# Softmax maxima of two of four heads by pairs of 64-row products, in groups of four, with scores and maxima in one ring of five PSUM banks

## The chip, the core and the metric

The kernel runs on one core of one Trainium2 chip. The metric is the time of one execution on the device in microseconds (us). The core has one engine for matrix products (TensorE, PE in the profile, with its weight loads as PEld) and three others that work on whole tiles: VectorE (DVE), ScalarE (ACT) and GpSimd (POOL). SyncE (SP) issues most DMAs. Each engine takes its instructions in the order in which they were written, and waits on semaphores for the others. PSUM, where TensorE writes, has eight banks of 128 partitions by 512 fp32 values.

## What is computed

One layer of a hybrid backbone: a modulated RMSNorm, one input projection, then grouped-query softmax attention (8 query heads, 2 key heads, head size 64) and, beside it, a bidirectional gated linear recurrence with 4 heads; an output projection, and a SwiGLU feed-forward layer. There are 2048 latent tokens and 256 context tokens, so attention runs over 2304 keys. What matters here is

```
def block(q):
    s = jnp.einsum('bqkgd,bnkd->bkgqn', q, keys).astype(jnp.float32) * scale
    p = jax.nn.softmax(s, axis=-1)
    return jnp.einsum('bkgqn,bnkd->bqkgd', p.astype(vals.dtype), vals)
```

The softmax subtracts a number per query and head from the scores before the exponential. In exact arithmetic the result does not depend on that number, as long as it is near the row's maximum.

## The kernel before

The kernel has an opening and the projection (to 709 us of the profile), the stage that holds attention and the recurrence together (to some 1620 us), and then the output projection and the feed-forward layer. The change lies in the second stage, and prepares for it in the first.

**Items and steps.** Attention runs over 32 items: for each of the two key heads (`g`) 16 blocks of 128 queries (`qt`), each with four query heads side by side, 512 columns. An item has 18 steps, one for each tile of 128 keys (`NKT` is 18). The loop at line 1407 counts `x` over all steps; `n` is the item and `k` the step in it.

**Operands in two parts.** Queries and keys are split into a high part that keeps fewer bits and a low part that holds the rest. `KS[g]` holds the keys, 64 rows of high part and under them 64 rows of low part; `qa` holds the high part of the queries twice, in both halves of the rows, so one 128-row product gives high query times whole key. `KB` holds the high part of the keys alone (rows 0 to 63) and a row of -1, `qb` the low part of the queries and, in that row, the maxima. The halves of the keys are made in `qk_side` (lines 590 to 603), written to `s_k`, and read by `load_kb` (line 1263) with one DMA for each third of the keys.

**A step.** `scores` (line 1182) takes a bank of `ps_st` (three banks, tag "s"), puts two 128x512 products into it (lines 1190 and 1191), and lets ACT take the exponential into `p` (line 1194). Then `chunk` (line 1151) makes a piece of the maxima that the next but one or the next item will need: a 128x512 product into a bank of `ps_mx` (two banks, tag "x") and on DVE the minimum along the row into `mn` (lines 1159 to 1161; signs are turned, so minima stand for maxima). An item has 18 chunks: 16 for the four heads by four blocks of 512 latent keys, and two (16 and 17) for the last 256 keys of two heads each. `CHUNKS` (line 1383) puts them at steps -10 to 7 of the item before, which is step 8 to 17 of the one before that and 0 to 7. With chunk 17 the twenty minima become four (`neg`, line 1171). At step 10 `maxima` (line 1173) turns `neg` with TensorE into a bank of the same pool (`pn`), ACT copies it to `mr`, and four DMAs put it into `qb`.

**A batch.** At step 10 an item's first batch, and at step 2 of the next item its second (`EVENTS`, line 1130), the loop at line 1488 first lets the recurrence compute a level (`rec.round`, products `pa`, line 818), then DVE adds one pair of exponentials (`SUMS`, letter E), then TensorE makes the products with the values and the sums (`products`, lines 1215 and 1223, tile `av`), and after that DVE does the masked copies of the level (line 831) and POOL its multiplications (`M`, `Q`, `C`, lines 847 to 855). Two POOL additions of 128x1024 go with each batch (line 1205).

**The recurrence.** Its work is placed by hand: `Recurrence` (line 995) gives every operation a step `x`, for head `h` at 18 x (4+7h) plus a fixed number (lines 739 to 743 and 1004 to 1029). So the stage repeats every seven items, and within the seven the steps carry different work. `level_context` (line 1050) does one level of the context's unit: a copy by ACT from `C` to `M` (line 844) and two multiplications by POOL.

**Order.** In the stage the orders of PE, DVE, ACT and POOL are those of the program (line 1460); only SP's is planned.

Of the kernel before, what the change touches and what calls it, by code (L numbers as in the profile page):

```python
# [38 lines left out]
P5M = False  # L39
WOV = (1, 3, 5, 7)  # L40
# [27 lines left out]
def block_kernel(ctx: ExitStack, tc: tile.TileContext, a: dict, out: bass.AP, dbg=None):  # L68
# [240 lines left out]
    with proj as st:  # L309
# [223 lines left out]
        def qk_side(t, c):  # L533
# [56 lines left out]
            else:  # L590
                sf = qp.tile([P, 512], F32R, tag="sk", name=f"s{name}", bufs=SK)
                sk = sf[:, :256].rearrange("p (g s d) -> p g s d", g=2, s=2)
                nc.scalar.activation(sk[:, :, 0, :], x, AF.Copy)
                nc.vector.tensor_tensor(sk[:, :, 1, :], x, f32v(sk[:, :, 0, :]), op=ALU.subtract)
# [118 lines left out]
    with ExitStack() as st:  # L713
# [413 lines left out]

        BATCHES = [[0, 8], [8, 18]]
# [3 lines left out]
        class Item:  # L1132
# [18 lines left out]
            def chunk(self, c):  # L1151

                if c == 0:
                    self.mn = sm.tile([P, 4, 5], F32, tag="mn", name=f"mn{self.nm}")
                s = ps_mx.tile([P, 512], F32, tag="x", name=f"mx{self.nm}_{c}")
                K = KS[self.g]
                if c < 16:
                    h, k = divmod(c, 4)
                    nc.tensor.matmul(s, self.qa[:, h * P:(h + 1) * P], K[:, k * 512:(k + 1) * 512],  # L1159
                                     start=True, stop=True)  # L1160
                    nc.vector.tensor_reduce(self.mn[:, h, k:k + 1], s, axis=AX.X, op=ALU.min)  # L1161
                else:
                    h = (c - 16) * 2
                    for i in range(2):
                        nc.tensor.matmul(s[:, i * 256:(i + 1) * 256], self.qa[:, (h + i) * P:(h + i + 1) * P],
                                         K[:, 2048:], start=True, stop=True)
                    nc.vector.tensor_reduce(self.mn[:, h:h + 2, 4], s.rearrange("p (h k) -> p h k", h=2),
                                            axis=AX.X, op=ALU.min)
                if c == 17:
                    self.neg = sm.tile([P, 4], F32, tag="neg", name=f"neg{self.nm}")  # L1170
                    nc.vector.tensor_reduce(self.neg, self.mn, axis=AX.X, op=ALU.min)

            def maxima(self):

                pm = ps_mx.tile([P, 512], F32, tag="x", name=f"pn{self.nm}")
                nc.tensor.transpose(pm[:4, :P], self.neg, ident)
# [5 lines left out]
            def scores(self, k):  # L1182
# [5 lines left out]
                s = ps_st.tile([P, 512], F32, tag="s", name=f"s{nm}")  # L1188
# [60 lines left out]
        QB = [qpl.tile([P, 512], F32R, name=f"qb{i}") for i in range(2)]  # L1249
        one32 = kvp.tile([P, 32], F32, name="one32")  # L1250
# [12 lines left out]
        def load_kb(g, r):  # L1263
            n = NTOK // 3
            nc.sync.dma_start(f32v(KB[r][:64, :]), s_k[g][:64, r * n:(r + 1) * n])
# [63 lines left out]
        def turn_heads(t, hs, eng, lag=0, ps=ps_h, tag="h"):  # L1329

            pt = ps.tile([P, 512], F32, tag=tag, name=f"mt{t}_{hs[0]}")
# [4 lines left out]
        def turn_first():  # L1336

            turn_heads(FIRST, [0, 1, 2], nc.vector, 1, ps_mx, "x")
            split_mix(FIRST, mixed[FIRST][0][:, :512], 0, 4, nc.gpsimd)
# [43 lines left out]
        CHUNKS = [-10, -9, -8, -7, -6, -5, -4, -3, -2, -1, 0, 1, 2, 3, 4, 5, 6, 7]  # L1383
        chunks, loads = {}, {}
        for n in range(1, NIT):
            for c in range(18):
                chunks.setdefault(NKT * (n - 1) + CHUNKS[c], []).append((n, c))

# [14 lines left out]
        for x in range(CHUNKS[0], 0):  # L1403
            for n, c in chunks.pop(x, ()):
                items[n].chunk(c)

        for x in range(NKT * NIT + 1):
# [65 lines left out]
            for m, c in chunks.pop(x, ()):  # L1473
                items[m].chunk(c)
# [13 lines left out]
            for e, t in enumerate(EVENTS):  # L1488
                m, r = divmod(x - t, NKT)
                if r or m < 0:  # L1490
                    continue
                made = rec.round() if e in ROUNDS else iter(())
                next(made, 0)
                for p in range(BATCHES[e][0] // 2, BATCHES[e][1] // 2):
                    if SUMS[p] in "EQ":
                        items[m].add(p)
                items[m].products(e)
# [3 lines left out]
                if TE == 9 and e in ROUNDS:  # L1501
                    for u in rec.lanes.values():
                        u.extend(u.lv)

# [701 lines left out]
```

## Time and profile before

| what | us |
|---|---|
| median of 3 runs | 3114.13 (3111.4 to 3115.98) |
| profiled execution | 3117.9 |
| its span, first to last instruction | 3116.1 |

The page of the profile adds up what each engine was busy. A window gives the same for a stretch of time. The groups give for one line and operation the count, the busy time and the mean duration of one; records of PE overlap, as the next product enters while the last one leaves, so what a product costs is read from the distance of two starts. The timeline gives instructions in order of time, neighbours of one kind merged, with the idle time in front and what ended it in square brackets. The view of waits adds up who waited for whom.

### The profile page before, as it was taken

Reading aid. Unit: us, or ns where it says so; the run is one execution under the profiler, and the core shown is the slowest. Engines: PE = TensorE matmul, PEld = TensorE weight load, DVE = VectorE, ACT = ScalarE, POOL = GpSimd, SP = SyncE. Lnnn points to the kernel's source line nnn. Section 1 sums busy time; section 2 is a strip of 40 time slices with the busy share of each in tenths; the row PEclk is TensorE's granted clock in tenths of the full one; section 3 lists DMA queues with packets and bytes.
Section 4 is the critical chain, followed back from the end, with each engine's and each line's share of the span. In section 5 each row is a group of like instructions: output and inputs, shape, how many; then the busy total and the mean of one; then the engine's idle time right before and its main releaser. Section 6 shows DMA issues by size and latency. Waiting matters only on the chain.

```text
span 3116.1 us, 51235 instructions
## 1 busy us (share of the span) xinstructions
PE 3074.8 (99%) x18844; PEld 2483.8 (80%) x18844; DVE 1845.9 (59%) x3252; ACT 1303.1 (42%) x2656; POOL 1602.7 (51%) x1291
## 2 busy tenths in 40 slices
PE   9999999999999999999999999999999999999999
PEld 7888888886777778777778878788888788888887
DVE  4554655427777787786745574544478743333567
ACT  4422322214545545555553253333345533333454
POOL 3311212106989888898862118676600277776122
PEclk9999999999999999999999999999999999999999
DMA  7544544425111212111124444656596533333765
GB/s 244 159 139 127 155 139 150 141 69 138 42 38 49 67 53 71 39 52 48 42 83 147 129 142 155 213 176 211 171 331 196 182 118 106 102 102 102 254 195 196
DMA packets 372998, 410.77 MB, mean 132 GB/s; under 512 B 34469, under 2 KB 264073, under 8 KB 372234
## 3 DMA queue, kind: packets, MB, share of 16 engines
q1 hardware_dynamic: 369722, 405.06, 41.0%
q8 instruction: 148, 2.42, 0.3%
q10 hardware_dynamic: 3024, 2.43, 0.2%
q14 instruction: 104, 0.85, 0.1%
HBM read 277.54 MB, written 133.97 MB: 132 GB/s over the span
## 4 chain that ended last, share of the span: by engine, by line
PE 70%; DVE 7%; DMA 5%; POOL 3%; issue 2%; ACT 1%; SPq 1%; POOLq 0%; DVEq 0%; ACTq 0%
PE pA L1785 13%; PE av L1215 7%; PE pB L1785 6%; PE y L1355 6%; PE pd0A L2082 4%; PE pd1A L2082 3%; PE s L1190 3%; PE s L1191 3%; PE pC L1785 3%; PE mx L1159 3%; PE i L442 2%; DVE mn L1161 2%; PE pd0B L2082 2%; PE pd1B L2082 2%; PE pa L818 2%
## 5 line engine op out<-in xcount | busy, mean ns | idle before, releaser
L1194 ACT ACTIVATE p<-s 128x512 f32<-128x512 f32 x576 | 338.2, 600 | 372.6 <-PE s L1191 358.1
L1161 DVE TENSOR_REDUCE mn<-mx 128x1 f32<-128x512 f32 x496 | 337.0, 689 | 175.2 <-PE mx L1159 172.3
L1215 PE MATMUL av<-p,VS 128*64 128x256 f32 x2304 | 259.9, 379 | 0.0
L1190 PE MATMUL s<-qa,K 128*128 128x512 f32 x576 | 244.1, 424 | 1.2 <-ACT p L1194 1.0
L1191 PE MATMUL s<-qb,KB 128*128 128x512 f32 x576 | 226.9, 394 | 0.0
L1215 PEld LDWEIGHTS av<-p,VS 128*64 128x64 f32 x2304 | 160.4, 137 | 75.3 <-issue 1.1
L1205 POOL TENSOR_TENSOR ps<-p,p 128x1024 f32<-128x1024 f32 x64 | 153.4, 2396 | 101.8 <-ACT p L1194 101.7
L1159 PE MATMUL mx<-K,qa 128*128 128x512 f32 x496 | 200.1, 404 | 2.4 <-DVE mn L1161 1.2
L435 PE MATMUL f<-hTh,wh 128*128 128x512 f32 (+1 forms) x640 | 188.1, 373 | 0.2 <-ACT ft L475 0.2
L1205 POOL TENSOR_TENSOR ps<-ps,p 128x1024 f32<-128x1024 f32 x64 | 153.1, 2392 | 12.0 <-ACT p L1194 10.6
L2019 DVE TENSOR_TENSOR dl<-dl,x 128x512 fp32r<-128x512 f32 x154 | 113.8, 765 | 66.5 <-ACT x L2012 64.9
L2012 ACT ACTIVATE x<-dl 128x512 fp32r<-128x512 f32 x154 | 95.9, 631 | 95.4 <-DMA dl<-s_hid0S 37.7
L852 POOL TENSOR_TENSOR Q<-Q,T 128x512 f32<-128x512 f32 x96 | 131.3, 1383 | 8.1 <-PE pa L818 7.7
L435 PEld LDWEIGHTS f<-hTh,wh 128*128 128x128 f32 x640 | 116.9, 190 | 20.4 <-ACT ft L475 0.3
L1190 PEld LDWEIGHTS s<-qa,K 128*128 128x128 f32 x576 | 109.0, 189 | 27.0 <-issue 12.3
L2012 ACT ACTIVATE dh<-dl 128x512 fp32r<-128x512 f32 x154 | 88.9, 624 | 98.7 <-PE pd1A L2082 42.2
L2019 DVE TENSOR_TENSOR dl<-dl,dh 128x512 fp32r<-128x512 f32 x154 | 105.5, 697 | 39.9 <-ACT dh L2012 37.7
L1159 PEld LDWEIGHTS mx<-K,qa 128*128 128x128 f32 x496 | 93.6, 189 | 38.0 <-DVE mn L1161 15.3
L131 POOL TENSOR_TENSOR rs_xf<-ms_xf,mhalf 128x1 f32<-128x1 f32 x16 | 9.9, 620 | 221.1 <-DVE ms_xf L129 218.5
L1191 PEld LDWEIGHTS s<-qb,KB 128*128 128x128 f32 x576 | 109.3, 190 | 14.9
L435 PE MATMUL f<-hTl,wh 128*128 128x512 f32 (+1 forms) x320 | 118.7, 371 | 0.0
L131 POOL TENSOR_TENSOR rs_qq<-ms_qq,mhalf 128x4 f32<-128x4 f32 x32 | 34.0, 1061 | 161.0 <-DVE ms_qq L129 160.3
(436 smaller groups left out, 8913.5 us busy)
## 6 DMA issues: line engine op xcount, KB each, us to landing
w<-in_w_gu_dram SPq DMA_DIRECT2D x88, 512.0 KB
wm<-in_w_mod_dram SPq DMA_DIRECT2D x24, 1024.0 KB
dl<-s_wT SPq DMA_DIRECT2D x88, 256.0 KB
dl<-s_wB SPq DMA_DIRECT2D x66, 256.0 KB
wq<-in_w_down_dram SPq DMA_DIRECT2D x44, 256.0 KB
s_wT<-wq SPq DMA_DIRECT2D x44, 256.0 KB
dl<-s_hid1S SPq DMA_DIRECT2D x44, 256.0 KB
dl<-s_hid0S SPq DMA_DIRECT2D x44, 256.0 KB
```

The lines of the kernel that those rows point to most:

```text
L435: nc.tensor.matmul(pm[:, :n], w[wi][:, k, c0:c0 + P], hT[b][hi][:, k, :], start=(k == 0 and i == 0), stop=(k == KT - 1 and i == 2))
L1159: nc.tensor.matmul(s, self.qa[:, h * P:(h + 1) * P], K[:, k * 512:(k + 1) * 512], start=True, stop=True)
L1161: nc.vector.tensor_reduce(self.mn[:, h, k:k + 1], s, axis=AX.X, op=ALU.min)
L1190: nc.tensor.matmul(s, KS[self.g][:, ks], self.qa, start=True, stop=False)
L1191: nc.tensor.matmul(s, KB[k // 6][:, k % 6 * P:(k % 6 + 1) * P], self.qb, start=False, stop=True)
L1194: nc.scalar.activation(self.pairs[p][:, o:o + 512], s, AF.Exp, scale=-1.0)
L1205: (nc.gpsimd if SUMS[p] in "PQ" else nc.vector).tensor_tensor(t, a, self.pairs[p], op=ALU.add)
L1215: nc.tensor.matmul(self.av[i * 64:(i + 1) * 64, :256], VS[k // 6][:, k % 6, :], self.pairs[k // 2][:, o:o + 256], start=(k == 0), stop=(k ...
L1355: nc.tensor.matmul(py, m[:, k, :], wo[k][w][hf], start=(k == 0 and i == 0), stop=(k == KT - 1 and i == 2), skip_group_check=True)
L1785: nc.tensor.matmul(acc, w[wi][:, k, :], x[xi][k], start=(start and k == 0 and i == 0), stop=(stop and k == KH - 1 and i == 2), skip_group_ ...
L2019: nc.vector.tensor_tensor(lo, f32v(lo), f32v(hi), op=ALU.subtract)
L2082: nc.tensor.matmul(cur[t], l[:, t * P:(t + 1) * P], r, start=(start and j == 0 and f == 0), stop=(stop and j == NHF - 1 and f == 2), skip_ ...
```

## The change

- In `qk_side` the two halves of the keys of a tile are written in turned order for some tiles: `flipped(t)` is 1 for tiles 4 to 7, 12 to 15 and 17. In `KS` the high part then stands in rows 64 to 127 for every second block of 512 latent keys, and for the last tile. `load_kb` reads each run of tiles with one order by a DMA of its own: 7 for 3.
- For chunks 0 and 1, now one for each of heads 0 and 1, four products of 64 rows take the place of four of 128: rows 0 to 63 for blocks 0 and 2, rows 64 to 127 for blocks 1 and 3, each into a bank of its own. They hold high query times high key alone. For heads 2 and 3 and for the last 256 keys the chunks (8 to 17) stay as they were.
- A group of four is issued at step 10 (chunk 0) and at step 2 (chunk 1), in front of the recurrence's products and the batch. Its four reductions on DVE come behind the batch's add and in front of the masked copies. The other ten chunks go to steps 12 to 17 and 4 to 7; steps 0, 1, 3, 8, 9 and 11 have none. The first item with maxima has its own list.
- Scores, maxima and `pn` take banks in turn from one ring of five (`bank`), in the order st, x, st, x, st.
- The reduction to four minima goes to the step after chunk 17, into the first four columns of a 128x128 tile, and `pn` is turned in full width.

```diff
+def flipped(t):
+
+    return t // 4 % 2 if t < 16 else t % 2
...
-                nc.scalar.activation(sk[:, :, 0, :], x, AF.Copy)
-                nc.vector.tensor_tensor(sk[:, :, 1, :], x, f32v(sk[:, :, 0, :]), op=ALU.subtract)
+                f = flipped(t)
+                nc.scalar.activation(sk[:, :, f, :], x, AF.Copy)
+                nc.vector.tensor_tensor(sk[:, :, 1 - f, :], x, f32v(sk[:, :, f, :]), op=ALU.subtract)
...
+        taken = [0]
+
+        def bank(name):
+
+            n = taken[0] = taken[0] + 1
+            pl, tag = ((ps_st, "s"), (ps_mx, "x"))[n % 5 % 2]
+            return pl.tile([P, 512], F32, tag=tag, name=name)
...
-                s = ps_mx.tile([P, 512], F32, tag="x", name=f"mx{self.nm}_{c}")
                 K = KS[self.g]
+                if c < 2:
+                    banks = [bank(f"mx{self.nm}_{c}{i}") for i in range(4)]
+                    for i, s in enumerate(banks):
+                        r = slice(i % 2 * 64, i % 2 * 64 + 64)
+                        nc.tensor.matmul(s, self.qa[r, c * P:(c + 1) * P], K[r, i * 512:(i + 1) * 512],
+                                         start=True, stop=True)
+                    return [(self.mn[:, c, i:i + 1], s) for i, s in enumerate(banks)]
+                s = bank(f"mx{self.nm}_{c}")
...
-                if c == 17:
-                    self.neg = sm.tile([P, 4], F32, tag="neg", name=f"neg{self.nm}")
-                    nc.vector.tensor_reduce(self.neg, self.mn, axis=AX.X, op=ALU.min)
+                if c == LAST_CHUNK:
+                    later(1, self.lowest)
+
+            def lowest(self):
+
+                nc.vector.tensor_reduce(neg_all[:, :4], self.mn, axis=AX.X, op=ALU.min)
...
-                pm = ps_mx.tile([P, 512], F32, tag="x", name=f"pn{self.nm}")
-                nc.tensor.transpose(pm[:4, :P], self.neg, ident)
+                pm = bank(f"pn{self.nm}")
+                nc.tensor.transpose(pm[:, :P], neg_all, ident)
...
-                s = ps_st.tile([P, 512], F32, tag="s", name=f"s{nm}")
+                s = bank(f"s{nm}")
...
         def load_kb(g, r):
-            n = NTOK // 3
-            nc.sync.dma_start(f32v(KB[r][:64, :]), s_k[g][:64, r * n:(r + 1) * n])
+            t0 = 6 * r
+            while t0 < 6 * r + 6:
+                t1 = t0
+                while t1 < 6 * r + 6 and flipped(t1) == flipped(t0):
+                    t1 += 1
+                rows = slice(64 * flipped(t0), 64 * flipped(t0) + 64)
+                nc.sync.dma_start(f32v(KB[r][:64, (t0 - 6 * r) * P:(t1 - 6 * r) * P]), s_k[g][rows, t0 * P:t1 * P])
+                t0 = t1
...
-        CHUNKS = [-10, -9, -8, -7, -6, -5, -4, -3, -2, -1, 0, 1, 2, 3, 4, 5, 6, 7]
+        CHUNKS = [(-8, 0), (2, 1)] + list(zip((-6, -5, -4, -3, -2, -1, 4, 5, 6, 7), range(8, 18)))
+        FIRST_CHUNKS = [(-1, c) for c in range(8, 17)] + [(2, 0), (6, 1), (7, 17)]
+        LAST_CHUNK = 17
...
+        def lowest(group):
+
+            for o, s in group or ():
+                nc.vector.tensor_reduce(o, s, axis=AX.X, op=ALU.min)
...
-            for m, c in chunks.pop(x, ()):
-                items[m].chunk(c)
+            if k not in (2, 10):
+                for m, c in chunks.pop(x, ()):
+                    lowest(items[m].chunk(c))
...
+                group = [v for i, c in chunks.pop(x, ()) for v in items[i].chunk(c)]
                 made = rec.round() if e in ROUNDS else iter(())
                 next(made, 0)
                 for p in range(BATCHES[e][0] // 2, BATCHES[e][1] // 2):
                     if SUMS[p] in "EQ":
                         items[m].add(p)
+                lowest(group)
                 items[m].products(e)
                 next(made, 0)
```

More of the change, by code (lines that the diff above doesn't have):

```diff
@@ L1249, in block_kernel @@
         QB = [qpl.tile([P, 512], F32R, name=f"qb{i}") for i in range(2)]
+        neg_all = kvp.tile([P, P], F32, name="neg")
+        nc.gpsimd.memset(neg_all, 0.0)
         one32 = kvp.tile([P, 32], F32, name="one32")
@@ L1327, in split_mix, with turn_heads @@
             eng.tensor_tensor(ml[:, k0:k1, :], pv, f32v(hv), op=ALU.subtract)
-        def turn_heads(t, hs, eng, lag=0, ps=ps_h, tag="h"):
-            pt = ps.tile([P, 512], F32, tag=tag, name=f"mt{t}_{hs[0]}")
+        def turn_heads(t, hs, eng, lag=0, pt=None):
+            if pt is None:
+                pt = ps_h.tile([P, 512], F32, tag="h", name=f"mt{t}_{hs[0]}")
             for i, h in enumerate(hs):
@@ L1336, in turn_first @@
         def turn_first():
-            turn_heads(FIRST, [0, 1, 2], nc.vector, 1, ps_mx, "x")
+            turn_heads(FIRST, [0, 1, 2], nc.vector, 1, bank(f"mt{FIRST}_0"))
             split_mix(FIRST, mixed[FIRST][0][:, :512], 0, 4, nc.gpsimd)
@@ L1382, in block_kernel @@
         extra.setdefault(X0 + 10, []).append((turn_first, ()))
[L1383 removed]
+        CHUNKS = [(-8, 0), (2, 1)] + list(zip((-6, -5, -4, -3, -2, -1, 4, 5, 6, 7), range(8, 18)))
+        FIRST_CHUNKS = [(-1, c) for c in range(8, 17)] + [(2, 0), (6, 1), (7, 17)]
+        LAST_CHUNK = 17
         chunks, loads = {}, {}
         for n in range(1, NIT):
[L1386 to L1387 removed]
+            for x, c in CHUNKS if n > 1 else FIRST_CHUNKS:
+                chunks.setdefault(NKT * (n - 1) + x, []).append((n, c))
         rec = Recurrence()
@@ L1402, in block_kernel @@
             load_v(0, r)
-        for x in range(CHUNKS[0], 0):
+        for x in range(-1, 0):
+            now[0] = x
             for n, c in chunks.pop(x, ()):
                 items[n].chunk(c)
+            for f, args in todo.pop(x, []):
+                f(*args)
+        def lowest(group):
+            for o, s in group or ():
+                nc.vector.tensor_reduce(o, s, axis=AX.X, op=ALU.min)
         for x in range(NKT * NIT + 1):
@@ L1503, in block_kernel @@
                         u.extend(u.lv)
+            for m, c in chunks.pop(x, ()):
+                lowest(items[m].chunk(c))
     with ExitStack() as st:
```

2 lines of the change are left out of this document (1 added, 1 removed).

## The prediction

> **What bounds the kernel now.** First the page's span, then the busy time of two stretches (columns: stretch and its length, then busy us of PE, PEld, DVE, ACT and POOL, instructions in brackets; then granted clock, DMA), then PE in order of time, then the waits.
>
> ```profile
> span 3116.1 us, 51235 instructions
> ```
>
> ```profile
> 780.00:1560.00 780.00, 775.16 (x7409) 592.93 (x7406) 599.84 (x977) 408.04 (x920) 689.25 (x559) 1.00 0.18 50
> 709.40:726.20 16.80, 15.08 (x48) 9.64 (x46) 14.19 (x23) 8.14 (x13) 4.25 (x2) 0.80 0.73 164
> ```
>
> In the attention stage (780 to 1560) PE is the bound, but POOL is close: 689 of 780 us, 88%. The second row is the stage's start, where PE idles and the granted clock falls to 0.80. The stage has 32 items of 18 steps, a step being one key tile; here is the end of the run of steps 3 to 10 in item 14, up to the recurrence's products `pa`, which open the batch:
>
> ```profile
> 1114.50 0.39 PE L1190 MATMUL s<-qa,K 128*128 128x512 f32 x1
> 1114.73 0.40 PE L1191 MATMUL s<-qb,KB 128*128 128x512 f32 x1
> 1114.96 0.40 PE L1159 MATMUL mx<-K,qa 128*128 128x512 f32 x1
> 1115.45 0.27 PE L1176 MATMUL pn<-identr,neg 128*4 128x128 f32 x1
> 1115.65 1.15 PE L818 MATMUL pa<-Q,M 128*64 128x64 f32 x32
> ```
>
> A record lasts 0.39, but the next starts 0.23 later: a 128x512 product costs 0.23 us of PE, and a step with a maximum 0.70. From the step's second score product (1114.73) to `pa` are 0.92 us, with 0.49 between `mx` and `pn` where 0.23 would do. DVE is the pace beside it. From the view of who waited for whom, PE's weight loads in the same stretch (us in total, times, longest):
>
> ```profile
> PEld mx L1159 <- DVE mn L1161: 9.6, 34, 0.6
> ```
>
> **The change, part by part.** I write A for the group that goes in at step 10 and B for that at step 2.
>
> *Pairs.* Eight 64-row products replace eight of 128 rows. No 64-row product is in this trace. The nearest row is the batch's group, with busy us and mean ns:
>
> ```profile
> L1215 PE MATMUL av<-p,VS 128*64 128x256 f32 x1968 | 221.8, 379 | 0.0
> ```
>
> 1968 records in 221.8 busy us are 0.113 each while one lasts 0.379, so two column halves run together. The other bound is that they take turns at 0.23. I take pairs of 0.23, as `av` is the nearest shape: per item 8 slots become 4, 0.92 us less; at the other bound nothing. [...] What a change of shape costs stands here:
>
> ```profile
> 1102.78 0.40 PE L1159 MATMUL mx<-K,qa 128*128 128x512 f32 x1
> 1103.10 1.15 PE L818 MATMUL pa<-Q,M 128*64 128x64 f32 x32
> ```
>
> 0.32 instead of 0.23 is 0.09 a switch; a group adds one in front, as the one to `pa` is paid already. For the signal that releases a bank I take 0.05 (POOL to ACT it is 0.02 below: 1176.64 to 1176.66).
>
> *The ring, and the new wait.* Five banks go round over scores, maxima and `pn`. At step 10 the order is score 10, `pn`, four maxima. So **the fourth product takes the bank of score 10, and waits for that step's exponential**; at step 2 the fourth waits for the exponential of step 1. Behind it on PE stand the rest of the group, `pa` and the whole batch, and POOL's `Q` and DVE's masked copy wait for `pa`. Before, `pa` needed none of these exponentials. When do they end? ACT in order of time, first in item 14, then in item 18:
>
> ```profile
> 1115.22 0.60 ACT L1194 ACTIVATE p<-s 128x512 f32<-128x512 f32 x1 [0.15 <-PE s L1191]
> ...
> 1225.90 1.10 ACT L1194 ACTIVATE p<-s 128x512 f32<-128x512 f32 x2
> ```
>
> An undisturbed one starts 0.49 after the second score product (1114.73) and takes 0.60; two in a row follow at 0.50.
>
> Plain A, from the second score product: the exponential ends at 1.09, the fourth product starts at 1.14, `pa` at 1.14+0.32 = 1.46 against 0.92. The run before it has lost the maxima of steps 3, 8 and 9, 0.69. Net -0.15 us. Plain B: step 1's exponential ends at -0.46+0.49+0.03+0.60 = 0.66, the fourth product starts at 0.71, `pa` at 1.03 against 0.23+0.32 = 0.55; steps 11, 0 and 1 lose 0.69. Net -0.21. Had PE not to wait, the fourth product would start at 0.23+0.20+0.23 = 0.66 in A (0.20 from `pn` to the next shape, as 1115.45 to 1115.65) and at 0.32+0.23 = 0.55 in B: -0.63 and -0.37.
>
> *Where ACT is held.* In some items POOL is late, and ACT, which takes its instructions in order, waits for POOL in front of exponential 10. So far nothing on PE stood behind that. ACT's row in the view of waits (780 to 1560), then item 16: POOL, ACT and PE in order of time:
>
> ```profile
> ACT M L844 <- POOL C L855: 16.4, 7, 6.3
> ```
>
> ```profile
> 1166.31 2.39 POOL L1205 TENSOR_TENSOR ps<-p,p 128x1024 f32<-128x1024 f32 x1 [3.60 <-ACT p L1194]
> ...
> 1176.22 0.42 POOL L855 TENSOR_TENSOR C<-M,T 128x128 f32<-128x128 f32 x1
> ```
>
> ```profile
> 1176.66 0.31 ACT L844 ACTIVATE M<-C 128x128 f32<-128x128 f32 x1 [3.11 <-POOL C L855]
> 1176.88 0.58 ACT L1194 ACTIVATE p<-s 128x512 f32<-128x512 f32 x1
> ```
>
> ```profile
> 1174.01 1.19 PE L818 MATMUL pa<-Q,M 128*64 128x64 f32 x28
> ```
>
> POOL begins at 1166.31, released by exponential 3, and reaches the context's `C` 9.9 us later; PE was at `pa` after 7.7. Exponential 10 ends at 1177.46, 3.45 after `pa` began. With the change `pa` waits for it: 1177.46+0.05+0.32 = 1177.83, **3.8 us later**. Nothing that the change removes lies in that POOL chain. The plan (line 1005) places a head's work at 18 x (4+7h) plus fixed steps, so it repeats every 7 items: 9, 16 and 23, 3 x 3.8 = 11.4. Three waits of 3.1 and the longest, 6.3 in item 2, make 15.6 of the row's 16.4. Item 2 and three smaller kinds, each with `pa` on PE and exponential 10 on ACT:
>
> ```profile
> 777.59 1.49 PE L818 MATMUL pa<-Q,M 128*64 128x64 f32 x32
> ...
> 782.92 0.59 ACT L1194 ACTIVATE p<-s 128x512 f32<-128x512 f32 x1
> ...
> 1143.80 1.19 PE L818 MATMUL pa<-Q,M 128*64 128x64 f32 x32
> ...
> 1144.12 0.59 ACT L1194 ACTIVATE p<-s 128x512 f32<-128x512 f32 x1
> ...
> 1210.15 1.04 PE L818 MATMUL pa<-Q,M 128*64 128x64 f32 x28
> 1210.35 0.59 ACT L1194 ACTIVATE p<-s 128x512 f32<-128x512 f32 x1
> ...
> 1226.75 1.15 PE L818 MATMUL pa<-Q,M 128*64 128x64 f32 x32
> ```
>
> Item 2: 783.51+0.37-777.59 = +6.3. Items 1, 8, 15, 22 (the context's preparation stands before exponential 10): it ends at 1144.71, comes some 0.6 earlier with shorter steps, so 1144.11+0.37-1143.80 = +0.7, four times 2.8. Items 10, 17, 24 (an output at step 9): 1210.94-0.69+0.37-1210.15 = +0.5, three times 1.5. Items 4, 11, 18, 25 have `psf` between score 10 and `pn`, no wait: 0.92 less, 0.46+0.09 more, -0.4 each, -1.6. The 15 plain A give -2.3. **A: +18.1.** B: 27 plain -5.7; three (into items 11, 18, 25, with an output's squares on ACT) like item 18, where the two exponentials from 1225.90 end at 1227.00 and `pa` came at 1226.75: 1227.00-0.23+0.37-1226.75 = +0.4, +1.2. **B: -4.5.**
>
> *DVE.* Its count stays; four reductions stand together behind the batch's own add, some 2.6 us, in front of the masked copies. They lie beside the batch. DVE's last before, and the next run's first score, at A in item 14:
>
> ```profile
> 1119.65 0.26 DVE L873 TENSOR_REDUCE T<-T 128x64 f32<-128x128 f32 x1
> 1120.77 0.50 PE L1190 MATMUL s<-qa,K 128*128 128x512 f32 x1
> ```
>
> DVE was done at 1119.91; with 2.6 more at 1122.5, and the next run's first maximum, of step 12, is there 1.0+0.4 after its first score, at 1122.2: nothing with two banks to spare, 0.3 a group where the cover is gone. Of the 9.6 us that weight loads waited for reductions I take 3 away (0 to 9.6), since steps 8 to 11 and 0 to 3 have none.
>
> *Start, loads, the rest.* The start is paced by DVE:
>
> ```profile
> 710.41 3.25 DVE L1161 TENSOR_REDUCE mn<-mx 128x1 f32<-128x512 f32 x5
> 716.78 0.63 PE L1190 MATMUL s<-qa,K 128*128 128x512 f32 x1
> ```
>
> ```profile
> 702.31 1.91 SPq L1265 DMA_DIRECT2D KB<-s_k  x3
> ```
>
> Ten reductions stood before the first score; with nine maxima in five banks it starts after five. 18 reductions of 0.65 from 710.41 end at 722.1, so the first batch (726.20, where the second window above ends) comes 2 to 3 earlier: -2.5 (0 to -3). `KB` takes 7 issues on SP for 3, four times 0.64, before the high queries' row with `m0` at the start: hidden, as the scores start at 714; 2.6 if not. The reduction to `neg` moves from step 7 to 8, two steps ahead of `pn`. The swapped halves of `K` and the full-width `pn` add no instruction; the memset of `neg` is one, on POOL, before the stage.
>
> Sum: 18.1 - 4.5 - 3 - 2.5 = **+8**, against the profiled execution's 3117.9 (span 3116.1 and 1.8 around it), 0.3%. The median is 3114.1, 3.8 lower; I add the difference there: **3122**.
>
> [...]
>
> [...]
>
> **Rivals.** *The hold does not reach the groups* (20%, faster). Place: exponential 10 of items 2, 9, 16, 23. Price: 17.7 us; 8 - 17.7 = -10, 3104 (3093 to 3108, with the plain waits gone too at the low end). It decides for faster once the hold is under half, that is if POOL's chain ends 2 us earlier or the banks come in another order. Against it: the chain starts at an exponential that the change does not bring forward. *The pairs take turns* (18%): the change does not do what it says. Plain B's fourth product comes at 0.32+0.69 = 1.01 for 0.71, so 27 x 0.3 = 8, and the four A with `psf` 0.46 each: +18, 3132. For it: no row of the trace. Against it: `av`. *No wait in plain groups* (20%): exponentials come early enough, A gains 0.48 and B 0.16 more, 15 x 0.48 + 27 x 0.16 = 11: -3, 3111. Against it: 0.60 of exponential for 0.46 of score products.
>
> **How the numbers follow.** The forecast (42%) spans 3116 to 3128, from the bounds of DVE's waits (3 and 9.6), the start and a late DVE. About 0.2%, 6 us, can be told from no change. Faster: 0.19 of the first rival and 0.05 of the third, 0.24. Slower: 0.30 of the forecast and the 0.18, 0.48. Within: 0.28. The range 3095 to 3135 leaves out the first rival's low end and the second's high end.
>
> **What would show it.** Right: PE waits for ACT `p` at line `mx`, some 17 us in four items, the longest over 3 us, and `pa` of item 16's kind 3 to 4 us later; second products of a pair starting under 0.03 us after the first. Wrong: no wait of PE over 1 us on ACT; group products 0.23 apart; or waits of scores for DVE, which would mean that the four reductions, not ACT, are late.

## The result, and the profile after

The changed kernel takes 3138.9 us (median of 5 runs, 3137.7 to 3142.8), the kernel before 3114.7 (5 runs): 1.0077 times as long, 95% interval 1.0061 to 1.0092. It is slower by 24 us, where 8 were forecast, and lies above the range. The profiled execution took 3139.7.

Of the changed kernel: the page's first line, then two stretches that answer to those shown of before (stretch and length, busy us of PE, PEld, DVE, ACT and POOL, instructions in brackets, granted clock, DMA), then the view of waits of 780 to 1560 (us in total, times, longest).

```profile
span 3137.9 us, 51328 instructions
```

```profile
780.00:1560.00 780.00, 759.07 (x7210) 568.38 (x7207) 567.38 (x946) 382.19 (x892) 667.25 (x543) 0.99 0.17 48
704.97:719.81 14.84, 13.45 (x50) 7.01 (x48) 12.74 (x22) 8.26 (x14) 4.77 (x2) 1.00 0.81 183
```

```profile
PE mx L1174 <- ACT p L1218: 16.7, 9, 4.3
...
PEld mx L1174 <- ACT p L1218: 31.8, 44, 4.7
```

PE's busy time between 780 and 1560 fell from 775 to 759 us: PE now stands still, and the line that it waits at is the forecast one, the groups' products (L1174; line numbers are those of the changed kernel now) for exponentials. The longest of these waits, 5.4 us in item 2, ends at 777.76, just ahead of this view. Item 16 in order of time, PE, POOL, DVE and ACT of the changed kernel:

```profile
1183.16 0.39 PE L1215 MATMUL s<-qb,KB 128*128 128x512 f32 x1
1183.39 0.27 PE L1200 MATMUL pn<-identr,neg 128*128 128x128 f32 x1
1183.60 0.73 PE L1174 MATMUL mx<-K,qa 64*128 64x512 f32 x3
1188.59 0.79 PE L1174 MATMUL mx<-K,qa 64*128 64x512 f32 x1 [4.26 <-ACT p L1218]
1189.31 1.98 PE L824 MATMUL pa<-Q,M 128*64 128x64 f32 x32
```

```profile
1183.63 2.35 POOL L1229 TENSOR_TENSOR ps<-ps,p 128x1024 f32<-128x1024 f32 x1
1185.94 0.41 POOL L853 TENSOR_TENSOR M<-M,T 128x128 f32<-128x128 f32 x1
1186.32 1.40 POOL L861 TENSOR_TENSOR C<-M,T 128x128 f32<-128x128 f32 x1
```

```profile
1186.02 1.42 DVE L1229 TENSOR_TENSOR ps<-ps,p 128x1024 f32<-128x1024 f32 x1 [1.15 <-POOL ps L1229]
1187.36 1.87 DVE L1448 TENSOR_REDUCE mn<-mx 128x1 f32<-128x512 f32 x3
```

```profile
1187.74 0.31 ACT L850 ACTIVATE M<-C 128x128 f32<-128x128 f32 x1 [4.34 <-POOL C L861]
1187.96 0.58 ACT L1218 ACTIVATE p<-s 128x512 f32<-128x512 f32 x1
```

The chain is the one forecast: `C` on POOL lets ACT copy, then exponential 10 runs to 1188.54, and 0.05 later the fourth product starts. Two things were not forecast. `C` lasts 1.40 where it lasted 0.42 before, because DVE's add began 0.3 ahead of it. And `pa` comes 0.72 behind the fourth product, not 0.32. The granted clock (the last but two of the columns) in three stretches, with the wait in the first, shows what fell together with it:

```profile
1183.00:1188.50 5.50, 1.33 (x7) 0.56 (x6) 4.35 (x7) 1.07 (x5) 5.42 (x6) 0.79 0.20 51
1188.50:1193.10 4.60, 4.51 (x43) 3.23 (x45) 2.96 (x6) 0.81 (x4) 4.19 (x5) 0.51 0.01 1
1193.10:1196.10 3.00, 3.00 (x40) 1.78 (x36) 0.00 (x0) 0.00 (x0) 1.87 (x3) 1.00 0.11 14
```

After the wait PE works at half clock for 4.6 us. To see what that makes, I cut each item at four points: from the first score product of step 3 to the first `pa` (run A), from there to the first score product of step 11 (batch A), then the same at step 2 of the next item (run B, batch B). Item 16 has its step 3 at 1164.85 before and 1175.21 after, `pa` at 1174.01 and 1189.31, step 11 at 1179.33 and 1196.16: run A 9.16 and 14.10, batch A 5.31 and 6.85. The sums over the stage, from the two profiled executions, in us, after less before:

| stretch | items | forecast | measured |
|---|---|---|---|
| run A | 9, 16, 23 | +11.4 | +14.6 |
| run A | 2 | +6.3 | +6.7 |
| run A | 1, 8, 15, 22 (context's preparation) | +2.8 | +3.6 |
| run A | 10, 17, 24 (output) | +1.5 | +1.8 |
| run A | 4, 11, 18, 25 (`psf`) | -1.6 | -0.4 |
| run A | the rest, plain | -2.3 | -0.2 |
| run A | 0 | 0 | +1.2 |
| batch A | 2, 9, 16, 23 | 0 | +7.2 |
| run B | all | -4.5, and -3 for DVE's waits | -0.2 |
| batch B | 15 and 22 | 0 | -2.5 |
| start, to step 3 of item 0 | | -2.5 | -7.6 |
| sum | | +8 | +24.2 |

The sum ends at step 11 of the last item. Behind it 2.3 us are given back, and the two spans differ by 21.8; that the sum equals the difference of the medians, 24.2, is chance.

Of the start's 7.6 us, 4.4 are there before the stage begins. The projection's last addition on DVE, before and after:

```profile
710.07 0.42 DVE L454 TENSOR_TENSOR ie<-ie,i 128x256 f32<-128x256 f32 x1 [2.40 <-ACT ie L453]
```

```profile
705.64 0.42 DVE L459 TENSOR_TENSOR ie<-ie,i 128x256 f32<-128x256 f32 x1 [2.40 <-DMA KB<-s_k]
```

Its wait is 2.40 in both, so the load of `KB` that the second row names does not delay it. In the profiles of the other kernels with the change it starts between 703.9 and 707.3. Of the kernel before there is one profile, whose execution was 3.8 slower than its median, so it stays open how much of the 4.4 is the change and how much is chance. From there to step 3 of item 0 are 10.1 before and 7.0 after.

### The profile page after: what moved, and what is told of

Read it like the earlier page. It is cut to its first block, busy times and chain, and to the rows that moved or that the text cites. A ratio compares the mean times of both kernels' runs of the same rounds, so it can differ in the third digit from the quotient of the medians.

```text
span 3137.9 us, 51328 instructions
## 1 busy us (share of the span) xinstructions
PE 3077.3 (98%) x18844; PEld 2472.2 (79%) x18844; DVE 1830.5 (58%) x3252; ACT 1289.4 (41%) x2656; POOL 1599.0 (51%) x1292
## 4 chain that ended last, share of the span: by engine, by line
PE 87%; DVE 3%; ACT 3%; POOL 2%; issue 2%; DMA 2%; SPq 0%; ACTq 0%; POOLq 0%; DVEq 0%
PE pA L1833 14%; PE av L1239 8%; PE pB L1833 7%; PE f L440 6%; PE y L1388 6%; PE s L1214 4%; PE pd1A L2130 3%; PE s L1215 3%; PE pC L1833 3%; PE pd0A L2130 3%; PE hq L440 2%; PE pa L824 2%; PE q L447 2%; PE g L447 2%; PE pd1B L2130 2%
## 5 line engine op out<-in xcount | busy, mean ns | idle before, releaser
L1218 ACT ACTIVATE p<-s 128x512 f32<-128x512 f32 x576 | 326.5, 602 | 425.0 <-PE s L1215 417.7
L1182 DVE TENSOR_REDUCE mn<-mx 128x1 f32<-128x512 f32 x248 | 168.8, 690 | 136.7 <-PE mx L1180 134.5
L1448 DVE TENSOR_REDUCE mn<-mx 128x1 f32<-128x512 f32 x248 | 153.7, 677 | 1.6 <-PE mx L1174 1.6
L1229 DVE TENSOR_TENSOR ps<-ps,p 128x1024 f32<-128x1024 f32 x64 | 103.3, 1615 | 49.5 <-POOL ps L1229 49.5
L1833 PE MATMUL pB<-x,S1h 128*128 128x512 f32 x352 | 110.7, 396 | 3.8 <-ACT S1h L1802 3.8
L2097 POOL TENSOR_TENSOR y<-y,yg 128x512 f32<-128x512 f32 x24 | 40.5, 1705 | 144.9 <-DVE yg L2096 118.5
```

What stands on the lines that cost most here:

```text
L1218: nc.scalar.activation(self.pairs[p][:, o:o + 512], s, AF.Exp, scale=-1.0)
L1229: (nc.gpsimd if SUMS[p] in "PQ" else nc.vector).tensor_tensor(t, a, self.pairs[p], op=ALU.add)
L1833: nc.tensor.matmul(acc, w[wi][:, k, :], x[xi][k], start=(start and k == 0 and i == 0), stop=(stop and k == KH - 1 and i == 2), skip_group_ ...
```

## The experiments

The theory from the two traces: the loss is the wait of the fourth product for exponential 10, made longer by DVE's add beside POOL's `C`, and the half clock that follows. The rival: the groups' own work costs, as pairs, changes of shape or reductions. The kernel before was run again with each series; its medians lay between 3110.8 and 3114.7. So a few us between kernels of different series are not told by the times alone, and stretches of the profiles stand beside them.

**pn behind the batch.** With `pn` out of the way, the fourth product takes the bank of score 9.

```diff
             rec.step(x)
-            if k == 10 and n + 1 < NIT:
-                items[n + 1].maxima()
...
             for m, c in chunks.pop(x, ()):
                 lowest(items[m].chunk(c))
+            if k == 10 and n + 1 < NIT:
+                items[n + 1].maxima()
```

> The changed kernel with one move: the transpose pn stands behind the batch of step 10 instead of in front of the group of four. The four products then take the banks that come behind score 10's, the fourth takes score 9's, and nothing on PE waits for exponential 10 before the batch. Theory 1 (the loss is the wait for exponential 10 where ACT is held, plus the half clock after PE has stood still for it): the four held items give back 14.6 + 6.7 us of run and 5.2 + 2.0 us of batch, the items with the context's preparation 3.6, those with an output 1.8, and the plain groups some 0.3 each, 17 times, 5: 39 in all, 3138.9 becomes 3100 (3097 to 3108), faster than the kernel before. Theory 2 (the groups' own work costs: pairs that do not overlap, the change of shape, four reductions together): only the plain waits go, 3125 to 3139.

Measured: 3109.1 (10 runs), 0.9986 of before (0.9976 to 0.9996). 30 us go, of the 39 expected, and the time lies 1 above the expected range. Runs A fall by 38.3 and batches A by 4.4 against the changed kernel, but 10.3 come back in runs B and 4.5 in batches B. Of these, 6.9 and 3.2 lie behind items 9, 16 and 23: there ACT is now late at exponential 1 of the next item, and the group at step 2 waits for it (shown below). Another 3.1 lie in runs B of items 8, 15 and 22, whose cause was not looked for, and 1.3 in the batch B of item 8, where an add of DVE lasts 6.53 (such adds are shown below). As the cause of the loss the rival is out.

**Full rows.** The same groups with 128-row products.

```diff
-                        r = slice(i % 2 * 64, i % 2 * 64 + 64)
+                        r = slice(0, P)
```

> The changed kernel with the pairs undone: the four products of a group read all 128 rows, one after the other, and give the exact maxima. Theory 1 (the fourth product waits for an exponential, so PE's time in front of it is hidden): 3138.9 stays within 4 us: 0.46 more a group only in the four with psf between and in a few others, +2, and 0.1 less from the fourth product to pa in the rest, -5. Theory 2 (PE's own work sets the group): 62 groups x 0.46 = 28 us more, 3167.

Measured: 3143.7 (4 runs), 1.0095 (1.0080 to 1.0110): 4.7 more, just over the 4 of the first theory and far from the 28 of the second. Most of it is 0.13 in each plain run B (2.1 in 16) and 0.25 in each run A of the four with `psf` (1.0). Runs A of the other kinds but item 0 do not move: there the wait hides PE's work.

**A filler.** PE repeats the third product through the wait.

```diff
+        FILL = {4: 22, 11: 18, 18: 18, 25: 18}
...
+                        for _ in range(FILL.get(self.n, 1) if c == 0 and i == 2 else 1):
-                        nc.tensor.matmul(s, self.qa[r, c * P:(c + 1) * P], K[r, i * 512:(i + 1) * 512],
-                                         start=True, stop=True)
+                            nc.tensor.matmul(s, self.qa[r, c * P:(c + 1) * P], K[r, i * 512:(i + 1) * 512],
+                                             start=True, stop=True)
```

> The changed kernel, where the third product of the group is written 18 times (22 in item 2) in the four held items alone, so that PE works through the wait for exponential 10 and does not stand still. The wait itself stays. Theory 1: the granted clock stays at 1.0 through the batch; the batches come back from 2.0 + 5.2 us longer to no longer, and the step from the fourth product to pa from 0.72 to 0.43: 3138.9 becomes 3131 (3129 to 3134), with 70 products more. Theory 2 (the batch is longer because of late adds or reductions, not of the clock): the same time as the changed kernel, 3139, or longer.

Measured: 3127.1 (4 runs), 1.0041 (1.0026 to 1.0056). That is 2 below the expected range. The batches of the four items are 5.31 long again, 7.3 less in all, and the runs give 1.7 more. Of these 9.0 some 8 are the clock's: in item 2 the run is 1.2 shorter, and 1.0 of that is `C`, which lasts 0.41 in this profile and 1.39 in that of the changed kernel. The rest of the gain, some 3 us, lies outside the attention's stretches (start 1.2). The kernel with the filler, in the same wait of item 16 and the batch behind it:

```profile
1176.00:1181.50 5.50, 5.08 (x23) 3.57 (x22) 4.30 (x8) 1.09 (x4) 5.42 (x7) 1.00 0.16 48
1181.50:1187.00 5.50, 5.47 (x77) 3.83 (x81) 2.81 (x6) 0.76 (x3) 5.50 (x6) 1.00 0.02 3
```

The fourth product comes no earlier than exponential 10 allows, but the clock stays at 1.00, and `pa` follows it by 0.43 in place of 0.72. With 72 products more the kernel is 12 us faster. `C` on POOL and the add on DVE in item 2 of this kernel:

```profile
774.02 0.41 POOL L861 TENSOR_TENSOR C<-M,T 128x128 f32<-128x128 f32 x1
```

```profile
773.72 1.80 DVE L1231 TENSOR_TENSOR ps<-ps,p 128x1024 f32<-128x1024 f32 x1 [3.94 <-POOL ps L1231]
```

**Reductions ahead of the add**, in the four held items.

```diff
+                if e == 0 and n in (2, 9, 16, 23):
+                    lowest(group)
+                    group = ()
                 for p in range(BATCHES[e][0] // 2, BATCHES[e][1] // 2):
```

> The changed kernel, where in the four held items DVE's four reductions stand ahead of the batch's own add at step 10 instead of behind it. Theory 1 (the hold is longer than forecast because the add, come forward, runs beside POOL's C and M and stretches them from 0.42 to 1.40 us): C ends 0.7 to 1.0 earlier, exponential 10 with it, PE stands still 3.7 to 3.9 us instead of 4.6; 3138.9 becomes 3135 (3131 to 3137), more if the clock then holds. Rival (POOL's C is long by itself there, or released late): the same time.

Measured: 3120.7 (6 runs), 1.0032 (1.0020 to 1.0044): 18 us less, where 4 were expected. The reason is another one. In item 16 the fourth product starts at 1174.39, 0.05 after the group's own first reduction ends and 1.5 before exponential 10 starts. So, with the reductions ahead, building the program has given the fourth product another bank, one that this reduction frees; how banks are dealt out there was not looked into. The row of waits of this kernel (700 to 1640) that the changed kernel does not have:

```profile
PEld mx L1174 <- DVE mn L1448: 6.3, 4, 1.6
```

So the time says nothing of the add, but the run takes the wait on exponential 10 away by itself: runs A lose 14.6 in the four items, batches A 7.3; 2.5 come back in run B. The trace does speak of the add: where it starts behind `C`, in items 9, 16 and 23, `C` lasts 0.40 to 0.43 again.

**The add of pair 3 on DVE**, in the four held items.

```diff
-                (nc.gpsimd if SUMS[p] in "PQ" else nc.vector).tensor_tensor(t, a, self.pairs[p], op=ALU.add)
+                (nc.gpsimd if SUMS[p] in "PQ" and (self.n not in (2, 9, 16, 23) or p != 3) else nc.vector).tensor_tensor(t, a, self.pairs[p], op=ALU.add)
```

> The changed kernel, where in the four held items the add of pair 3 (steps 6 and 7, 2.35 us on POOL ahead of the context's M and C) goes to DVE. Theory 1 (POOL's chain from exponential 3 to C sets exponential 10, which sets the fourth product): the chain is 2.3 us shorter, exponential 10 ends some 2.5 earlier, PE stands still about 2 us, so its clock does not fall either: each held item gives back 2.5 + 0.4 + 1.3 to 2.4, in all 18: 3121 (3117 to 3128). Rival (the hold comes from ACT's or the context's own order, not from POOL's queue): within 4 us of 3139.

Measured: 3131.7 (4 runs), 1.0069 (1.0053 to 1.0084): 7 less, not 18, and between theory and rival. The held runs are 1.5 shorter each (2.6 in item 2), not 2.5, and the clock falls as before. POOL's two `Q` in item 16 beside the add that came to DVE:

```profile
1174.52 3.55 POOL L804 TENSOR_TENSOR Q<-q,F 128x512 f32<-128x512 f32 x2
```

```profile
1174.76 2.14 DVE L1229 TENSOR_TENSOR ps<-ps,p 128x1024 f32<-128x1024 f32 x1 [1.09 <-ACT p L1218]
```

Two `Q` take 2.6 elsewhere (1.30 each); here the second starts when DVE's add lets it. What POOL was relieved of, it partly waited out; further on in item 16 it waits 0.81 and 0.69 for DVE, which now is late.

**No add on DVE in the held items**, with reductions out of PSUM in its place, so that the banks stay; PE sums that pair.

```diff
+        BARE = {2: (2,), 9: (2,), 16: (2,), 23: (2,)}
...
-                for p in [p for p in range(k0 // 2, k1 // 2) if SUMS[p] == "."]:
+                for p in [p for p in range(k0 // 2, k1 // 2) if SUMS[p] == "." or p in BARE.get(self.n, ())]:
...
-                    if SUMS[p] in "EQ":
+                    if SUMS[p] in "EQ" and p not in BARE.get(m, ()):
                         items[m].add(p)
+                    elif SUMS[p] == "E":
+                        for _ in range(6 if m == 2 else 3):
+                            nc.vector.tensor_reduce(scrap, group[2][1], axis=AX.X, op=ALU.min)
```

> The changed kernel, where in the four held items DVE's add of pair 2 at step 10 is left out of DVE (PE sums that pair with the products by ones: 8 more, some 0.46 us in the batch) and in its place DVE reduces the third product's bank three times into a scrap column (six times in item 2), so that each tile keeps its bank and the fourth product still waits for exponential 10. Theory 1 (the hold is longer than forecast because DVE's add, which reads two operands in SBUF, keeps POOL's C from starting: 1.40 us for 0.42): beside reductions out of PSUM C takes 0.42 again, exponential 10 ends 0.8 to 1.0 earlier, and each held run is that much shorter, 3 to 4 us in all, less 1.8 for the products by ones: 3137 (3134 to 3139); PE still stands still for some 3.7 us, so its clock still falls. Rival (C is long for its own reasons or for the late M): C at 1.40, runs as in the changed kernel, 3141.

Measured: 3134.5 (4 runs), 1.0072 (1.0056 to 1.0087). Its profiled execution started 1.7 later; in its items the runs are 0.97, 0.97, 1.28 and 1.06 shorter, and little else moves but the batches A, which are 1.9 longer, with the products by ones in them. POOL and ACT of this kernel in item 16:

```profile
1186.18 0.42 POOL L853 TENSOR_TENSOR M<-M,T 128x128 f32<-128x128 f32 x1
1186.55 0.42 POOL L861 TENSOR_TENSOR C<-M,T 128x128 f32<-128x128 f32 x1
```

```profile
1187.22 0.58 ACT L1220 ACTIVATE p<-s 128x512 f32<-128x512 f32 x1
```

`C` is back at 0.42 and exponential 10 comes 3.35 behind the start of POOL's add (1183.87 there), against 4.33 in the changed kernel. That is the theory's number, and the time lies in its range.

**The group split**: one pair in front of the batch, one behind it, on top of `pn` behind the batch; and the same with full rows.

```diff
...
-                group = [v for i, c in chunks.pop(x, ()) for v in items[i].chunk(c)]
+                which = chunks.pop(x, ())
+                group = [v for i, c in which for v in items[i].chunk(c, (0, 1))]
...
                 items[m].products(e)
+                rest = [v for i, c in which for v in items[i].chunk(c, (2, 3))]
                 next(made, 0)
+                lowest(rest)
```

> The kernel with pn behind the batch (3109.1), and the group split: one pair in front of pa, the other behind the batch, ahead of pn; its two reductions follow DVE's masked copies. Then no product in front of a batch takes a bank younger than two steps' scores. Theory 1 (what is left of the loss are waits of the fourth product for exponentials 1 and 9): the three waits of 2.3 to 2.7 us in front of the B groups of the items with the hold go, 7, and about 0.3 in each plain group, while a switch of shape more costs 0.1 to 0.2 in each: 3100 (3095 to 3106). Rival (POOL's chain is late whatever PE does, and the wait moves on to scores 11 to 13 or to the next products of the recurrence): 3106 to 3112.

> The split kernel with 128-row products in place of the pairs (the maxima are then of the whole products). Where nothing waits for exponentials, PE's own work shows: 62 groups, in each two pairs of about 0.23 to 0.33 become four products of 0.23, 0.46 more, less some 0.2 for the changes of shape: +16 against the split kernel (+10 to +28). Rival (PE is not what sets these groups even then): within 4 us of the split kernel.

Measured: 3108.9 (10 runs), 0.9993 (0.9983 to 1.0002), and 3109.9 (10 runs), 0.9997 (0.9987 to 1.0006). Neither is faster than `pn` moved alone. The groups' waits are gone, and with a pair moved out of each run, runs A and B together are 26.7 shorter than with `pn` moved alone; but 26.6 come back in the batches, where the pair behind a batch costs 0.43 in most. A whole group in front of the batch is as good where it does not wait. Full rows cost 16 by the first theory and 1 by measurement, within the rival's 4. Three long adds of DVE (see below) stood in the first profile and none in the second; without these 5 us the stretches are 1.4 longer with full rows, 0.02 a group.

**Split only where the hold reaches the group at step 2**, and with full rows.

```diff
...
+                cut = 2 if e == 1 and n in (10, 17, 24) else 4
...
```

> The kernel with pn behind the batch (3109.1) with the split in three groups alone, those at step 2 behind the items with the hold, where 2.4 to 2.7 us of waiting for exponential 1 are left and the granted clock fell to 0.62 behind it. From the split kernel's own stretches: 8.8 us of run and 1.9 of batch go, the second pair behind the batch costs 0.43 each, the plain groups stay as they are: 3109.1 - 9.5 = 3100 (3097 to 3104), some 0.35% faster than the kernel before. Rival (each wait taken away appears again later in the item, since POOL is late whatever PE does): 3106 to 3110.

> The same kernel with 128-row products in place of the pairs (whole products for the maxima). If a pair is worth 0.23, 62 groups x 2 give +28 less what waits hide. From the plain group without a wait in the changed kernel, 0.82 us from its first product to pa against 3 x 0.23 + 0.32 = 1.01: 0.19 a group, 62 times, +12 at most against the split-held kernel, and +4 to +10 as half of the groups still wait for exponential 9. Rival (the changes of shape take all that pairs save, as the split kernels' equal times suggest): within 3 us.

Measured: 3105.7 (8 runs, 3100.5 to 3111.5), 0.9976 (0.9966 to 0.9987), and 3107.7 (10 runs), 0.9983 (0.9974 to 0.9992). The first lies above the expected 3097 to 3104, and full rows cost 2.0 more, within the rival's 3. The three waits go (-8.8 in run B, -1.9 in batch B, against `pn` moved alone). Here is one of them, in the kernel with `pn` moved alone, and the clock behind it:

```profile
979.74 0.50 PE L1174 MATMUL mx<-K,qa 64*128 64x512 f32 x1 [1.98 <-ACT p L1218]
```

```profile
979.70:984.20 4.50, 4.46 (x47) 3.12 (x49) 3.69 (x9) 1.10 (x3) 3.44 (x5) 0.62 0.21 62
```

But the profiled execution of the split, the slowest of its eight, lost some 4.9 in items 11 and 18 each (3.4 and 3.8 in the batch, the rest in run B), where the change of this run does nothing. DVE and POOL of that kernel at item 11:

```profile
1029.63 6.95 DVE L1229 TENSOR_TENSOR ps<-ps,p 128x1024 f32<-128x1024 f32 x1 [0.48 <-POOL ps L1229]
```

```profile
1029.56 1.05 POOL L853 TENSOR_TENSOR M<-M,F 128x256 f32<-128x256 f32 x1
1030.56 0.64 POOL L853 TENSOR_TENSOR M<-M,T 128x256 f32<-128x256 f32 x1
1031.16 1.81 POOL L858 TENSOR_TENSOR Q<-Q,F 128x512 f32<-128x512 f32 x1
...
1034.87 0.64 POOL L861 TENSOR_TENSOR C<-M,T 128x256 f32<-128x256 f32 x1
```

An add of 1.2 us lasted 6.95, until POOL had been through six operations (the last ends at 1035.5). PE waited 3.3 for it, and the clock fell to 0.68. In the profile with full rows the add of item 11 took 2.02; without what items 11, 15, 18 and 22 lost to such adds, the stretches are some 6 longer with full rows. Before had two such adds, at 1157.90 (5.89) and in item 22; the changed kernel has none, which is the -2.5 of batch B in the table.

**Without those adds.** PE sums pair 2 of items 4, 11, 18, 25 and pair 7 of items 8, 15, 22 itself.

```diff
+        BARE = {4: (2,), 11: (2,), 18: (2,), 25: (2,), 8: (7,), 15: (7,), 22: (7,)}
...
-                for p in [p for p in range(k0 // 2, k1 // 2) if SUMS[p] == "."]:
+                for p in [p for p in range(k0 // 2, k1 // 2) if SUMS[p] == "." or p in BARE.get(self.n, ())]:
...
-                    if SUMS[p] in "EQ":
+                    if SUMS[p] in "EQ" and p not in BARE.get(m, ()):
                         items[m].add(p)
```

> The split-held kernel (3105.7) without the DVE adds that were found locked out behind POOL for 6.5 to 7.0 us in some executions: pair 2 of items 4, 11, 18, 25 and pair 7 of items 8, 15, 22 are summed by PE's products by ones, 0.46 us each, 3.2 in all. Theory (these lock-outs cost 1.3 us each where the batch covers most of the add and some 5 where it doesn't, in some executions and not in others): the spread of 3100.5 to 3111.5 shrinks, no add lasts over 3 us in the attention stage, and the median is 3102 (3099 to 3105). Rival (the lock-outs pass to other adds, or their cost lies beside other work): 3106 to 3110.

Measured: **3096.7** (5 runs, 3095.5 to 3099.0), 0.9953 of before (0.9940 to 0.9965): faster than both kernels, and 2 below the expected range. Between 780 and 1560 no add of DVE lasts over 2.04 (view of the tile, min, median and max in ns), and PE's only row of waits there is this:

```profile
L1231 DVE TENSOR_TENSOR ps<-ps,p x48: 1216/1630/2041, 784.7 to 1544.8; 128x1024 f32<-128x1024 f32 x48
```

```profile
PE s L1216 <- DVE mn L1184: 1.2, 3, 0.4
```

Not all of the gain is lock-outs that are gone. In items 4 and 25 the split's profile had none, and their runs B fall by 1.3 and 1.6 all the same. The likeliest reason is that DVE has more time for its reductions, for which PE's waits fall from 4.8 to 1.2 between 780 and 1560; no run sets this apart.

**The pairs by themselves**: that kernel with full rows (the one-line edit above).

> The kernel without the lock-outs (3096.7) with 128-row products in place of the pairs (whole products for the maxima): what pairs are worth where nothing else disturbs. If a pair saves the 0.23 that the prediction took, 0.46 a group less 0.1 for two changes of shape, 62 groups: +22, 3119, and at least +15 where some still wait. If the load of the second pair's weights and the changes of shape take most of it (0.335 from pair to pair, 0.42 from the last product to pa, in the changed kernel's trace): 0.1 to 0.2 a group, +6 to +12, 3103 to 3109.

Measured: 3100.7 (5 runs), 0.9964 (0.9950 to 0.9977): 4.0 more than with pairs, less than either expectation, and 7.6 more from first to last score of the stage. So a group of two pairs is worth some 0.07 to 0.12 us here, not the 0.46 of the forecast. The 4.0 compares two series, and the intervals of the two ratios overlap; the 7.6 compares two profiles.

## Why the prediction was wrong

**The side and the mechanism were right.** The fourth product of a group waits for the exponential that held ACT; PE's waits at that line are 18.2 us in the four held items, 4.3 each in three and 5.4 in item 2, and 4.9 in seven other places; `pn` moved behind the batch takes them away and leaves 6.6 at step 2.

**The step that failed is the price of the hold**: "3.8 us later", and with it the 17.7 of the four held items. They cost 21.3 in their runs and 7.2 in their batches, 28.5. In item 16 the 3.8 became 4.94 in the run, and 1.5 more in the batch. Two terms make most of the difference.

First, "Nothing that the change removes lies in that POOL chain" was false. The reductions of steps 8, 9 and 10 stood on DVE in front of its add, and held it until POOL's `C` was through. The last of them on DVE before, to be set against the row of `C` (1176.22, 0.42) in the prediction:

```profile
1175.15 0.68 DVE L1161 TENSOR_REDUCE mn<-mx 128x1 f32<-128x512 f32 x1
1175.75 0.94 DVE L1233 RECIPROCAL ot<-ot 128x128 f32<-128x128 f32 x1
1176.61 1.16 DVE L1205 TENSOR_TENSOR ps<-ps,p 128x1024 f32<-128x1024 f32 x1
```

Without them DVE stood ready (its add waited 1.15 for POOL's add), started 0.3 ahead of `C` and kept it from running. Before, the same add kept the next `M` waiting instead (1.32 at 1176.71), one operation behind the one that mattered. From the start of POOL's first add (1166.31 and 1176.65) to exponential 10 are 10.57 before and 11.31 after, 0.74 more: `C` lasts 0.98 longer and starts 0.24 sooner. The same holds for items 9 and 23; in item 2 `C` lasted 1.40 before too. The run without the add gave 0.97 to 1.28 back.

Second, there was no term for PE's clock. Behind the 4.3 us of standing still it was 0.51 for 4.6 us; in the filler kernel, where products fill most of that wait (PE busy for 5.08 of 5.50 us), it stayed at 1.00. From the fourth product to `pa` are then 0.72 for 0.32, 0.40 more, and the batch costs 1.3 to 2.4 more. Of the 0.40 the clock makes 0.29, as the filler kernel, at 1.00, has 0.43; the other 0.11 comes with the 64-row products, see below. 3.8 + 0.74 + 0.40 = 4.94. The filler showed the clock's part apart from the wait: some 8 of the 28.5. The start's row of the prediction had a clock of 0.80 in it, next to PE's idle time, and it was read as a property of the start. With that row (PE busy for 15.08 of 16.80 us) and the forecast wait of over 3 us, a term for the clock could have been put in as an estimate. Waits shorter than these 4.3 us were followed by a lower clock too (1.98 us by 0.62, last section).

**Pairs**: two products do start together, as forecast, but a pair does not take 0.23. The group at step 2 of item 14 of the changed kernel, rows that end with the second, the third and the fourth product, and `pa`:

```profile
1114.03 0.50 PE L1174 MATMUL mx<-K,qa 64*128 64x512 f32 x2
1114.03 0.73 PE L1174 MATMUL mx<-K,qa 64*128 64x512 f32 x3
1114.03 0.89 PE L1174 MATMUL mx<-K,qa 64*128 64x512 f32 x4
1114.86 0.34 PE L824 MATMUL pa<-Q,M 128*64 128x64 f32 x4
```

From the first product to `pa` are 0.83. The forecast had 0.71 with the wait for exponential 1, and 0.23 + 0.32 = 0.55 without one; four full products have 1.01. The third product, which lasts 0.39, ends at 0.73, so it starts 0.34 behind the first, 0.11 later than forecast. Whether the load of the second pair's weights holds it, the runs do not say. `pa` starts 0.42 behind the fourth product, not 0.32; by as much plain B falls short of its forecast.

**Plain groups.** A was forecast at -0.15 and measured at 0.0. From the second score product of item 14 (1125.78) `pa` came 1.63 later, 1.46 forecast: exponential 10 follows exponential 9 and starts 0.06 later than an undisturbed one, and `pa` comes 0.43 behind the last product instead of 0.32.

```profile
1125.78 0.39 PE L1215 MATMUL s<-qb,KB 128*128 128x512 f32 x1
1126.01 0.27 PE L1200 MATMUL pn<-identr,neg 128*128 128x128 f32 x1
...
1127.41 0.27 PE L824 MATMUL pa<-Q,M 128*64 128x64 f32 x1
```

Plain B gave half of its forecast (-0.11 each of 16, -0.21 forecast); the B with an output came as forecast (+1.5 for +1.2). Wrong were the B of items 4, 11, 18 and 25, +0.8 each, taken as plain; and the -3 for DVE's waits came to nothing in sum. Runs B of items 1, 8, 15 and 22, where maxima had waited for reductions, are 3.0 shorter, but scores now wait for reductions too, in the B of items 4, 18 and 25:

```profile
PE s L1214 <- DVE mn L1182: 3.4, 3, 1.2
```

Such waits were a sign of being wrong in the prediction; they are there, but small beside ACT's. **The start** came to -3.1 without the 4.4 that stood there before the stage, -2.5 forecast; PE did not wait for `KB`'s loads. **The rivals**: that the hold does not reach the groups did not come true, but two runs made it true. With `pn` moved the sign turned, as was said, though by less (3109 for 3104, 0.14% faster than before); with the reductions ahead the hold was gone too, but the kernel stayed 0.3% slower: the held runs are still 6.7 longer than before, with the fourth product waiting for a reduction. Pairs that take turns are ruled out, and plain groups do wait.

## What to carry to other kernels

A wait that an engine has in front of a long batch is priced with what comes behind it: here the clock that fell behind 18.2 us of waiting cost some 8 us more, and 72 useless products in the gaps were cheaper. Before work is taken off an engine, see what that work kept apart: here reductions kept a DVE add with two operands in SBUF from running into POOL's `C` (in item 16 0.42 us with them in front, 1.40 without). Where banks go round in a ring, write down the bank of every product in front of a batch with the instruction that frees it; one that stands behind another engine's chain does not belong there.

## What the runs showed of the hardware

Where DVE's add of two tiles in SBUF and operations of POOL met in the cases shown here, the one or the other lasted longer: `C` 1.40 for 0.42 (item 16 of the changed kernel), two `Q` 3.55 for 2.6 (item 16 of the run with the add of pair 3 on DVE), and the add 6.95 for 1.2 (item 11 of the split where the hold reaches). With reductions out of PSUM on DVE in the add's place, `C` lasted 0.42 (item 16 of the run without the add). An add that comes second was at times not let in between POOL's operations. In item 16 of the changed kernel it starts 0.08 behind the start of an `M` and gets in ahead of `C` (1.42); in item 2 of the filler kernel, at the same 0.08, it gets in only behind `C` (1.80); in item 11 of the split, at 0.07, it waits for six operations that follow without a gap (6.95). What decides stays open. Such cases may be why single executions of one kernel differ by several us (3100.5 to 3111.5).

PE's clock fell after waits far shorter than the 4.3 us of item 16. In the kernel with `pn` moved, 1.98 us of waiting were followed by 0.62 over 4.5 us. A longer wait, 2.29 at step 2 of item 17, left it at 1.00, and one of 2.33 at step 2 of item 24 was followed by 0.62 again; so it fell behind two of these three waits. With the add of pair 3 on DVE no single wait of PE in the 7 us in front of item 16's first batch was over 1.01, but PE was busy for 3.19 of 5 us, and the clock fell to 0.50:

```profile
1176.00:1181.00 5.00, 3.19 (x11) 1.67 (x11) 4.93 (x12) 2.00 (x7) 3.50 (x5) 0.78 0.19 56
1181.00:1185.50 4.50, 4.50 (x45) 3.19 (x46) 4.50 (x8) 0.28 (x1) 4.50 (x5) 0.50 0.01 1
```
